# Gram products of two heads issued in turn into two PSUM banks, and a task order planned with other durations

## The chip, the core and the metric

The kernel runs on one core of one Trainium2 chip. The metric is the device time of one execution in microseconds. Three runs of the kernel before took 3414.15, 3416.99 and 3423.1 us; the median is 3416.99.

## The reference, cut to what matters

Two layers over 512 latent tokens with 256 context tokens in front, width 1024. Layer 0 mixes by attention and convolution, layer 1 by RWKV-7, a recurrence over the tokens that runs once in each direction for 16 heads of 64 channels:

```python
def wkv_scan(state0, r, decay, k, a_vec, b_vec, v, reverse):
    def step(S, inp):
        r_t, w_t, k_t, a_t, b_t, v_t = inp
        sa = jnp.einsum('bhvk,bhk->bhv', S, a_t)
        S = S * w_t[:, :, None, :] + sa[..., None] * b_t[:, :, None, :] + v_t[..., None] * k_t[:, :, None, :]
        return S, jnp.einsum('bhvk,bhk->bhv', S, r_t)
```

The decay, k, a and b come out of small products (LoRA: 64 inner channels), sigmoids and exponentials of the layer's input. After the recurrence a readout with a group norm, a bonus term and a gate follows, and then a feed-forward block.

## The kernel before, in words

The kernel does the recurrence in chunks of 32 tokens, 24 chunks in each direction (8 of the context, 16 of the latent tokens). It goes in three steps: projections; a preparation (`rwkv_prep`) that needs no state; and the scan over the chunks (`rwkv_scan`). The change lies in the preparation.

The preparation works on 16 units u = 2m + d: m is one of 8 pairs of heads, d the direction. A pair of heads fills the 128 partitions: the first head (par = 0) has partitions 0 to 63, the second (par = 1) 64 to 127. For each pair it loads k and r (L2030, L2031) and normalises k (kk, L2044); for each unit it does the following.

- Two LoRA products into PSUM (pool `psa`), a tanh of each on ACT (L2070), a running sum over the tokens on DVE (`scan`, L2079 and L2081), and exponentials on ACT.
- DVE builds two tiles of 128 x 24 chunks x 64: `AR` (the decayed a and r, L2123 and L2127) and `KB` (the inversely decayed k and b, L2138 and L2142).
- TensorE forms for each head and chunk the 64 x 64 product of KB's chunk with AR's: the gram tiles (`gram`). One call fills one bank of `psa` with 12 chunks of one head: 6 side by side, and the two halves hf of the chunks on the two halves of the PSUM partitions. Four calls, (b, par) for b and par in 0, 1, make a unit. DVE masks each bank into the tile G (L2158).
- TensorE transposes KB (L2168, pool `psb`), ACT copies it into KT (L2171).
- AR, G and KT are spilled to DRAM by SP's queue (L2146, L2175, L2179), from where the scan loads them.

For each pair of heads there is also a bonus and gate part (L2244 to L2264) that ends in two stores to p_d (L2263, L2264); the work tiles of k, r, v and g are shared through small pools. After unit 7 a batch of triangular inverses (T, L2414 to L2483: 11 steps of rows and blocks, then 8 products and 8 sums, on DVE) starts for the first half of the heads, on what units 0 to 7 have spilled.

The order of all this is not written by hand. Every piece is a `task` with an engine (P, V, A, G, S for TensorE, DVE, ACT, GpSimd and SP), a duration in us, its dependences, what it takes and gives of the pools (`t` 15 tiles, `u` 5, `pa` and `pb` 4 banks each, `kb` and `kt` 2), a latency and a nominal unit. `run_tasks` is a list planner: it walks through time, starts on each free engine the ready task with the lowest priority number, and issues the instructions in that order. The priority is 3 times the unit, plus the earliest time by the durations, plus an offset for each kind of task from a table that stands in the call. On the chip every engine then takes its instructions in the order planned, and waits where an operand is not there.

Of the kernel before, what the change touches and what calls it, by code (L numbers as in the profile page):

```python
# [430 lines left out]
class K:  # L431
# [1534 lines left out]
    def rwkv_prep(self):  # L1966
        nc, A, dp = self.nc, self.A, self.dp
# [27 lines left out]
        def par_(n):  # L1995
            return slice(64 * n, 64 * n + 64)
# [17 lines left out]
        def tt(n):  # L2014
            return {"V": 0.1 + n / 960}

        def last(z, key, n):

# [5 lines left out]
        def head_tasks(m):  # L2024
            z = mz[m]
            u = 2 * m

            def load():
                z["k"], z["r"] = tt_("k"), tu_("r")
                nc.sync.dma_start(out=z["k"], in_=self.k_d[m])  # L2030
                nc.sync.dma_start(out=z["r"], in_=self.r_d[m])  # L2031

            def kn_p(i):
                if i == 0:
                    z["kk"] = tt_("kk")
                n = (512, 256)[i]
                ps = z["knp", i] = self.psb()
                for par in range(2):
                    h = 2 * m + par
                    self.mm(ps[par_(par), 0:n], self.cs[0:16, CC.at["ident"] + h:CC.at["ident"] + h + 1].to_broadcast([16, 64]), self.rn[i])  # L2040

            def kn_v(i):
                t0, n = ((0, 512), (512, 256))[i]
                nc.vector.scalar_tensor_tensor(z["kk"][:, t0:t0 + n], last(z, "k", 4)[:, t0:t0 + n], dcol[:, 56 + m:57 + m], z.pop(("knp", i))[:, 0:n], ALU.mult, ALU.mult)  # L2044

            task(("ld", m), "S", 1.82, load, [("bd", m - 2)], take=("t", "u"), u=u - 1, lat=2.2)
            for i in range(2):
                task(("knp", m, i), "P", (0.87, 0.45)[i], lambda i=i: kn_p(i), [("knp", m, 0), ("ld", m)], take=("pb",) + (("t",) if i == 0 else ()), u=u)
                task(("kk", m, i), "V", (0.66, 0.40)[i], lambda i=i: kn_v(i), [("knp", m, i), ("ld", m), ("cols",)], give=("pb", (("k", m), "t", 4)), u=u)

        def dir_tasks(u):
            m, d = u // 2, u % 2
# [104 lines left out]
            def gram_v(b, par):  # L2157
                nc.vector.tensor_tensor(G[:, 3 * b:3 * b + 3, par], z.pop(("g", b, par))[:, 0:384].rearrange("p (a s i) -> p a s i", a=3, s=2),  # L2158
# [21 lines left out]

            for w in "wa":
                for i in range(2):
                    task((w + "p", u, i), "P", (0.33, 0.65)[i], lambda w=w, i=i: lora_p(w, i), [(w + "p", u, 0), ("kb", u - 2)] + [("lo", 0 if w == "w" else 1), ("w2", 0 if w == "w" else 1)], take=("pa",) + (("t",) if i == 0 else ()), u=u - 0.5)
                    task((w, u, i), "A", (0.36, 0.57)[i], lambda w=w, i=i: lora_a(w, i), [(w + "p", u, i), ("cols",)], give=("pa",), u=u - 0.5, lat=0.25)
                if w == "w":
                    task(("half", u), "A", 0.83, half, [("w", u, 0), ("w", u, 1)], u=u, lat=0.25)
# [3 lines left out]
                    task(("wexp", u), "A", 1.36, wexp, [("dexp", u)], u=u, lat=0.25)  # L2190
            a = [("a", u, 0), ("a", u, 1)]
            task(("kb", u), "V", 0.87, k_b, a + kk, take=("t",), give=((("kk", m), "t", 6),), u=u)
            task(("kf", u), "A", 0.93, k_f, [("kb", u)], u=u, lat=0.25)
            task(("kd", u), "V", tt(768)["V"], lambda: k_d(nc.vector), [("kf", u), ("ld", m)], give=((("k", m), "t", 4),), u=u)
            old = [("z", d), ("sa", u - 2)] + [("g", u - 2, b, par) for b in range(2) for par in range(2)]
            for i in range(2):
                task(("ma", u, i), "V", (0.36, 0.66)[i], lambda i=i: mk_a(i), [("wexp", u)] + kk + old, give=((("kk", m), "t", 6), (("s", u), "t", 3)), u=u)
            task(("mr", u), "V", 0.64, mk_r, [("wexp", u), ("ld", m)] + old, give=((("s", u), "t", 3),), u=u)
            task(("me", u), "A", 0.2, mk_e, [("ld", m)] + old, u=u)
            ks = []  # L2200
            for i in range(len(pc)):
# [2 lines left out]
                ks.append(("mk", u, i))  # L2204
            for i in range(len(pc)):
                n = pc[i][3] - pc[i][2]
                task(("mb", u, i), "V", 0.1 + n / 960, lambda i=i: mk_b(i), [("kb", u), ("dexp", u), ("mk", u, 0)], give=((("dm", u), "t", 2 * len(pc)), (("b", u), "t", len(pc))), u=u)
# [12 lines left out]
            if u < 14:  # L2220
                task(("sk", u), "S", 2.2, spill_k, [("tc", u, b) for b in range(3)] + [("g", u, b, par) for b in range(2) for par in range(2)], give=("kt", "kb"), u=u, lat=2.2)
            else:
                self.late.append(spill_k)

        def bonus_tasks(m):
# [42 lines left out]
            task(("gp", m), "P", 0.65, gate, [("bd", m - 1), ("lo", 2), ("w2", 2)], take=("pb", "u"), u=u - 1)  # L2268
            task(("gc", m), "A", 0.48, gate_c, [("gp", m)], give=("pb",), u=u - 1, lat=0.25)
            task(("ba", m), "V", tt(512)["V"], lambda: add(nc.vector), ks, give=("t",), u=u)  # L2270
            task(("bm", m), "V", 0.66, mul, [("ba", m)] + [(n, 2 * m + d) for d in range(2) for n in ("mr", "me")], give=("t",), u=u)
            task(("bd", m), "P", 0.86, dot, [("bm", m)], take=("pb",), give=("u",), u=u)
            task(("b1", m), "V", 0.6, o1, [("bd", m), ("vl", m)], give=("pb",), u=u)
            task(("b2", m), "V", 0.66, o2, [("b1", m), ("gc", m)], u=u)
            task(("b3", m), "A", 0.61, o3, [("b2", m)], u=u, lat=0.25)
# [61 lines left out]
        for m in range(8):  # L2337
# [6 lines left out]
        self.run_tasks(tasks, dict(t=15, u=5, kb=2, kt=2, e2=2, pa=4, pb=4, raw=4, hi=1), eng, 3, 1.07, {'scan': -46.0, 'ld': -16.9, 'mask': -3.9, 'cols': -10.7, 'mr': -4.5, 'mb': -9.4, 'knp': -10.2, 'b1': 1.3, 'ap': -1.0, 'bs': 8.0, 'kk': -2.8, 'wp': -2.0, 'ba': -6.5, 'gc': -32.9, 'lh': 6.0, 'dexp': -2.2, 'll': -18.4, 'kb': -0.8, 'w2': 1.9, 'half': -4.7, 'vl': -11.4, 'kf': -0.1, 'gp': 3.9, 'z': -16.1, 'sg': -51.3, 'b3': -0.2, 'sa': 17.7, 'tp': -10.9, 'a': 0.9, 'lo': 34.2, 'T': 3.5, 'bd': -7.6, 'sk': 3.9, 'dm': 58.8, 'g': -8.5, 'b2': 3.0, 'mk': 0.4, 'wexp': -0.1, 'ma': -0.1, 'gv': -0.4, 'w': -0.4, 'bm': -0.2, 'tc': -0.1, 'kd': 1.6})  # L2344
        for u in (14, 15):
            del us[u]["KB"]
        w2.clear()
# [731 lines left out]
```

## Time and profile before

| what | value |
|---|---|
| median of three runs | 3416.99 us |
| profiled execution | 3418.43 us, span 3416.6 us |
| mean granted TensorE clock over the span | 0.937 |
| PE, DVE, ACT, POOL busy over the span | 92%, 65%, 34%, 14% |
| the preparation (read from the timeline) | from about 2415 us to about 2660 us of the span |
| gram instructions in it | 1536, 67.65 us busy |

Times in the profile are microseconds from the start of the span. An fp32 product shows as two MATMUL rows, so the 768 gram products are 1536 rows. PE busy is the time in which at least one product is in flight; products on different parts of the array can be in flight at the same time. The granted clock is 1.0 or 0.5 at any moment; a mean between them is a share of time.

### The profile page before, as it was taken

Reading aid. Unit: us, or ns where it says so; the run is one execution under the profiler, and the core shown is the slowest. Engines: PE = TensorE matmul, PEld = TensorE weight load, DVE = VectorE, ACT = ScalarE, POOL = GpSimd, SP = SyncE. Lnnn points to the kernel's source line nnn. Section 1 sums busy time; section 2 is a strip of 40 time slices with the busy share of each in tenths; the row PEclk is TensorE's granted clock in tenths of the full one; section 3 lists DMA queues with packets and bytes.
Section 4 is the critical chain, followed back from the end, with each engine's and each line's share of the span. In section 5 each row is a group of like instructions: output and inputs, shape, how many; then the busy total and the mean of one; then the engine's idle time right before and its main releaser. Section 6 shows DMA issues by size and latency. Waiting matters only on the chain. (4 is left out here: it accounts for less than half of the span.)

```text
span 3416.6 us, 53235 instructions
## 1 busy us (share of the span) xinstructions
PE 3157.3 (92%) x21616; PEld 2654.6 (78%) x21616; DVE 2215.4 (65%) x3658; ACT 1175.8 (34%) x2130; POOL 468.6 (14%) x362
## 2 busy tenths in 40 slices
PE   7999999988999999999999999998996478899999
PEld 6888888874578888888889988776665367678887
DVE  5877744797666776555767776637778675653433
ACT  4122113445533111213322323434654245532222
POOL 1000001366320000002000000216000142220000
PEclk9999999999999999999999999999755688989999
DMA  6444311200133444431111111232686888732222
GB/s 242 144 149 154 133 62 62 85 25 1 44 104 122 143 145 148 145 121 50 62 67 64 68 62 66 96 111 69 194 219 187 191 181 185 175 125 97 99 99 80
DMA packets 251382, 390.69 MB, mean 114 GB/s; under 512 B 67328, under 2 KB 136576, under 8 KB 251136
## 3 DMA queue, kind: packets, MB, share of 16 engines
q1 hardware_dynamic: 251136, 387.28, 36.7%
q8 instruction: 170, 2.79, 0.3%
q14 instruction: 76, 0.62, 0.1%
HBM read 323.24 MB, written 63.96 MB: 113 GB/s over the span
## 5 line engine op out<-in xcount | busy, mean ns | idle before, releaser
L528 PE MATMUL psa<-hhi,whi 128*128 128x512 f32 (+2 forms) x2296 | 797.1, 347 | 9.2 <-ACT whi L492 3.9
L528 PE MATMUL psa<-hlo,whi 128*128 128x512 f32 (+2 forms) x2296 | 798.1, 348 | 2.5 <-POOL hlo L680 2.3
L528 PE MATMUL psa<-hhi,wlo 128*128 128x512 f32 (+2 forms) x2296 | 795.7, 347 | 0.0
L499 DVE TENSOR_TENSOR wlo<-wraw,whi 128x1024 fp32r<-128x1024 f32 (+2 forms) x246 | 301.1, 1227 | 308.3 <-ACT whi L492 308.3
L528 PEld LDWEIGHTS psa<-hhi,whi 128*128 128x128 f32 x2296 | 436.1, 190 | 62.2 <-ACT whi L492 3.9
L528 PEld LDWEIGHTS psa<-hlo,whi 128*128 128x128 f32 x2296 | 435.7, 190 | 56.6 <-POOL hlo L680 4.2
L528 PEld LDWEIGHTS psa<-hhi,wlo 128*128 128x128 f32 x2296 | 435.9, 190 | 48.7
L528 PE MATMUL psb<-ghi,whi 128*128 128x256 f32 (+1 forms) x1232 | 428.7, 348 | 15.6 <-DVE xb L814 12.4
L528 PE MATMUL psb<-glo,whi 128*128 128x256 f32 (+1 forms) x1232 | 426.8, 346 | 0.9 <-DVE glo L377 0.2
L528 PE MATMUL psb<-ghi,wlo 128*128 128x256 f32 (+1 forms) x1232 | 426.0, 346 | 0.0
L492 ACT CAST whi<-wraw 128x1024 fp32r<-128x1024 f32 (+3 forms) x293 | 290.0, 1000 | 255.2 <-PE psb L528 103.7
L637 POOL TENSOR_TENSOR nacc<-nacc,nsq 128x512 f32<-128x512 f32 (+1 forms) x50 | 56.4, 1128 | 1576.1 <-ACT nsq L633 1571.2
L528 PEld LDWEIGHTS psb<-ghi,whi 128*128 128x128 f32 x1232 | 232.8, 189 | 49.0 <-DVE xb L814 13.8
L528 PEld LDWEIGHTS psb<-glo,whi 128*128 128x128 f32 x1232 | 232.7, 189 | 30.6 <-DVE glo L377 3.3
L528 PEld LDWEIGHTS psb<-ghi,wlo 128*128 128x128 f32 x1232 | 232.7, 189 | 29.9
L786 ACT CAST ghi<-fs 128x256 fp32r<-128x256 f32 (+1 forms) x118 | 63.0, 534 | 419.0 <-DVE fs L785 419.0
L777 ACT ACTIVATE fs<-psa 128x256 f32<-128x256 f32 (+1 forms) x116 | 59.5, 513 | 419.0 <-PE psa L528 419.0
L814 DVE SCALAR_TENSOR_TENSOR xb<-psb,mod,xb 128x256 f32<-128x256 f32 (+1 forms) x256 | 148.9, 611 | 51.4 <-PE psb L528 51.3
L563 DVE CUSTOM_DVE_ANT_0 adaj<-adat,sc,vec 128x512 bf16<-128x512 f32 x224 | 168.0, 750 | 15.0 <-DMA adat<-ada 9.3
L563 DVE CUSTOM_DVE_ANT_0 adaj<-adat,sc,mod 128x512 bf16<-128x512 f32 x224 | 168.0, 750 | 5.8 <-DMA adat<-ada 0.2
L528 PE MATMUL psb<-rhs,lhs 96*32 96x64 f32 (+1 forms) x2560 | 78.9, 237 | 70.6 <-DMA rhs<-v_d 39.6
L235 DVE TENSOR_TENSOR wlo<-wraw,whi 128x1024 fp32r<-128x1024 f32 x70 | 85.6, 1223 | 89.2 <-ACT whi L232 89.2
(422 smaller groups left out, 5381.8 us busy)
## 6 DMA issues: line engine op xcount, KB each, us to landing
wraw<-w SPq DMA_DIRECT2D x242, 512.0 KB
adat<-ada SPq DMA_DIRECT2D x256, 256.0 KB
la_d<-AR SPq DMA_DIRECT2D x32, 384.0 KB
kb_d<-KT SPq DMA_DIRECT2D x16, 768.0 KB
lg_d<-G SPq DMA_DIRECT2D x32, 384.0 KB
lhs<-la_d SPq DMA_DIRECT2D x48, 256.0 KB
lhs<-lg_d SPq DMA_DIRECT2D x48, 256.0 KB
kb<-kb_d SPq DMA_DIRECT2D x48, 256.0 KB
```

What stands on the lines that cost most here:

```text
L235: TT(lo, x, hi, ALU.subtract)
L492: nc.scalar.copy(hi, raw)
L499: nc.vector.tensor_tensor(lo, raw, hi, ALU.subtract)
L528: self.last = self.nc.tensor.matmul(ps, lhsT=lhsT, rhs=rhs, start=start, stop=stop)
L563: nc.vector.tensor_tensor_reduce(out=junk, in0=t, in1=self.sc[cd][hf], scale=1.0, scalar=o if hf else self.col("ada_b", l * 72 + j), op0=A ...
L637: (eng or nc.gpsimd).tensor_tensor(st["acc"], st["acc"], sq, ALU.add)
L777: nc.scalar.activation(s, ps[:, 0:grp[1]], AF.Silu)
L786: nc.scalar.copy(ghi[:, t0:t0 + n], s)
L814: nc.vector.scalar_tensor_tensor(xs, ps[:, 0:n], self.modc(l, gd, m, cd), xs, ALU.mult, ALU.add)
```

## The change

There are two parts. `gram` now takes two banks at once, one for each head of the pair, and issues the 24 products of both heads in turn: for each chunk first the head on partitions 0 to 63, then the one on 64 to 127. The two calls of one b become one task that takes two `pa` banks; the evictions stay separate, each giving one bank back, and both depend on the joint task. The number of products, their shapes and what they write are the same.

The second part changes the durations that the planner reckons with (TensorE tasks become up to twice as long, DVE and ACT tasks about 0.1 us longer, `scan` 1.75 us and not 0.95) and replaces the table of offsets. Each engine has the same number of instructions as before.

```diff
-            return {"V": 0.1 + n / 960}
+            return {"V": 0.15 + n / 960}
...
-            def gram(b, par):
-
-                ps = z["g", b, par] = self.psa()
-                p = par_(par)
+            def gram(b):
+
+                ps = [self.psa(), self.psa()]
+                z["g", b, 0], z["g", b, 1] = ps
                 for a in range(6):
                     for hf in range(2):
                         n = 12 * hf + 6 * b + a
-                        self.mm(ps[64 * hf:64 * hf + 64, 64 * a:64 * a + 64], z["KB"][p, n, :], AR[p, n, :])
+                        for par in range(2):
+                            p = par_(par)
+                            self.mm(ps[par][64 * hf:64 * hf + 64, 64 * a:64 * a + 64], z["KB"][p, n, :], AR[p, n, :])
...
-                    task((w + "p", u, i), "P", (0.33, 0.65)[i], lambda w=w, i=i: lora_p(w, i), ...
+                    task((w + "p", u, i), "P", (0.6, 1.1)[i], lambda w=w, i=i: lora_p(w, i), ...
...
-                    task(("scan", u), "V", 0.95, scan, [("half", u), ("mask",)], take=("t",), give=("t",), u=u)
+                    task(("scan", u), "V", 1.75, scan, [("half", u), ("mask",)], take=("t",), give=("t",), u=u)
...
             for b in range(2):
+                task(("g", u, b), "P", 1.7, lambda b=b: gram(b), ks + mar, take=("pa", "pa"), u=u)
                 for par in range(2):
-                    task(("g", u, b, par), "P", 0.8, lambda b=b, par=par: gram(b, par), ks + mar, take=("pa",), u=u)
-                    task(("gv", u, b, par), "V", 0.53, lambda b=b, par=par: gram_v(b, par), [("g", u, b, par), ("sg", u - 2)], give=("pa",), u=u)
+                    task(("gv", u, b, par), "V", 0.55, lambda b=b, par=par: gram_v(b, par), [("g", u, b), ("sg", u - 2)], give=("pa",), u=u)
             for b in range(3):
-                task(("tp", u, b), "P", 0.44, lambda b=b: trans(b), ks + [("tp", u, 0)], take=("pb",) + (("kt",) if b == 0 else ()), u=u)
+                task(("tp", u, b), "P", 0.85, lambda b=b: trans(b), ks + [("tp", u, 0)], take=("pb",) + (("kt",) if b == 0 else ()), u=u)
...
-        self.run_tasks(tasks, dict(t=15, ...), eng, 3, 1.07, {'scan': -46.0, 'ld': -16.9, 'mask': -3.9, ...})
+        self.run_tasks(tasks, dict(t=15, ...), eng, 3, 1.07, {'scan': -31.6, 'ld': -101.4, 'mask': -96.3, ...})
```

Three places of the new order follow. The lines of the changed kernel are two higher from the gram task on.

TensorE, the first two gram tasks of unit 0 (AR_20696 is the AR tile of direction 0, AR_20697 of direction 1; lh and ll are LoRA inputs; rows with KB and cs are the transposes). Before:

```order
L2168 MATMUL psb<-cs,KB 128x128 x4
L528 MATMUL psa<-lh_20715,whi 128x256
L528 MATMUL psa<-ll_20716,whi 128x256
L528 MATMUL psa<-lh_20715,wlo 128x256
L2168 MATMUL psb<-cs,KB 128x128 x8
L528 MATMUL psa<-AR_20696,KB 64x64 x48
L2168 MATMUL psb<-cs,KB 128x128 x12
L528 MATMUL psa<-AR_20697,KB 64x64 x48
```

Now:

```order
L528 MATMUL psa<-AR_20696,KB 64x64 x24
L528 MATMUL psa<-lh_20717,whi 128x256
L528 MATMUL psa<-ll_20718,whi 128x256
L528 MATMUL psa<-lh_20717,wlo 128x256
L2170 MATMUL psb<-cs,KB 128x128 x4
L528 MATMUL psa<-lh_20717,whi 128x512
L528 MATMUL psa<-ll_20718,whi 128x512
L528 MATMUL psa<-lh_20717,wlo 128x512
L528 MATMUL psa<-AR_20696,KB 64x64 x24
```

The 48 products of unit 0 stood in one run, a head at a time, behind its transposes. Now they come in two runs of 24, each of both heads, before and between the transposes, with LoRA products of other units in between.

SP's queue, around the load of k and r of the last pair of heads (the only L2030 and L2031 rows here). Before:

```order
L2179 DMA kb_d<-KT 128x12x128
L2175 DMA lg_d<-G_20699 64x6x256 x2
L2263 DMA p_d<-g 128x512
L2264 DMA p_d<-v 128x512
L2263 DMA p_d<-g 128x512
L2264 DMA p_d<-v 128x512
L2030 DMA k<-k_d 128x768
L2031 DMA r<-r_d 128x512
L2233 DMA v<-vt_d 128x512
L2146 DMA la_d<-AR_20696 64x12x128 x2
```

Now:

```order
L2146 DMA la_d<-AR_20696 64x12x128 x2
L2181 DMA kb_d<-KT 128x12x128
L2030 DMA k<-k_d 128x768
L2031 DMA r<-r_d 128x512
L2181 DMA kb_d<-KT 128x12x128
L2177 DMA lg_d<-G_20699 64x6x256 x2
L2146 DMA la_d<-AR_20697 64x12x128 x2
L2265 DMA p_d<-g 128x512
L2266 DMA p_d<-v 128x512
```

The load stood behind the p_d stores of pairs 5 and 6, and now stands ahead of both, with spills of units 11 to 13 between.

DVE, the last steps of the batch of triangular inverses (prod, tinv, tw) among the last units' work. Before (its last steps stand between the G rows of units 14 and 15, near the end of the preparation):

```order
L2158 TENSOR_TENSOR G_20698<-psa,cs 128x3x128 x2
L2478 TENSOR_REDUCE tinv<-prod 128x16x4
L2158 TENSOR_TENSOR G_20699<-psa,cs 128x3x128
L2474 TENSOR_TENSOR prod<-tw,tinv 128x1024
L2158 TENSOR_TENSOR G_20699<-psa,cs 128x3x128 x3
L2478 TENSOR_REDUCE tinv<-prod 128x16x4 x3
L2254 TENSOR_TENSOR v<-psb,v 128x512
```

Now (the KB rows are those of units 14 and 15):

```order
L2476 TENSOR_TENSOR prod<-tw,tinv 128x1024
L2127 TENSOR_TENSOR AR_20697<-r,s 128x16x31
L2160 TENSOR_TENSOR G_20699<-psa,cs 128x3x128 x2
...
L2480 TENSOR_REDUCE tinv<-prod 128x16x4 x3
L2114 TENSOR_TENSOR a<-a,k 128x768 x2
L2138 TENSOR_TENSOR KB<-a,dm 128x24x32
L2142 SCALAR_TENSOR_TENSOR KB<-b,dm 128x24x32
```

The batch ended behind the last unit's gram evictions and now ends before the last two units' KB tiles are built. Counted in DVE's 287 tasks it ran from the 199th to the 285th, and now runs from the 177th to the 267th.

More of the change, by code (lines that the diff above doesn't have):

```diff
@@ L2047, in head_tasks @@
             for i in range(2):
-                task(("knp", m, i), "P", (0.87, 0.45)[i], lambda i=i: kn_p(i), [("knp", m, 0), ("ld", m)], take=("pb",) + (("t",) if i == 0 else ()), u=u)
-                task(("kk", m, i), "V", (0.66, 0.40)[i], lambda i=i: kn_v(i), [("knp", m, i), ("ld", m), ("cols",)], give=("pb", (("k", m), "t", 4)), u=u)
+                task(("knp", m, i), "P", (0.95, 0.5)[i], lambda i=i: kn_p(i), [("knp", m, 0), ("ld", m)], take=("pb",) + (("t",) if i == 0 else ()), u=u)
+                task(("kk", m, i), "V", (0.74, 0.48)[i], lambda i=i: kn_v(i), [("knp", m, i), ("ld", m), ("cols",)], give=("pb", (("k", m), "t", 4)), u=u)
         def dir_tasks(u):
@@ L2182, in dir_tasks @@
                 for i in range(2):
-                    task((w + "p", u, i), "P", (0.33, 0.65)[i], lambda w=w, i=i: lora_p(w, i), [(w + "p", u, 0), ("kb", u - 2)] + [("lo", 0 if w == "w" else 1), ("w2", 0 if w == "w" else 1)], take=("pa",) + (("t",) if i == 0 else ()), u=u - 0.5)
-                    task((w, u, i), "A", (0.36, 0.57)[i], lambda w=w, i=i: lora_a(w, i), [(w + "p", u, i), ("cols",)], give=("pa",), u=u - 0.5, lat=0.25)
+                    task((w + "p", u, i), "P", (0.6, 1.1)[i], lambda w=w, i=i: lora_p(w, i), [(w + "p", u, 0), ("kb", u - 2)] + [("lo", 0 if w == "w" else 1), ("w2", 0 if w == "w" else 1)], take=("pa",) + (("t",) if i == 0 else ()), u=u - 0.5)
@@ L2185, in dir_tasks @@
+                    task((w, u, i), "A", (0.47, 0.69)[i], lambda w=w, i=i: lora_a(w, i), [(w + "p", u, i), ("cols",)], give=("pa",), u=u - 0.5, lat=0.25)
                 if w == "w":
-                    task(("half", u), "A", 0.83, half, [("w", u, 0), ("w", u, 1)], u=u, lat=0.25)
-                    task(("scan", u), "V", 0.95, scan, [("half", u), ("mask",)], take=("t",), give=("t",), u=u)
+                    task(("half", u), "A", 0.94, half, [("w", u, 0), ("w", u, 1)], u=u, lat=0.25)
+                    task(("scan", u), "V", 1.75, scan, [("half", u), ("mask",)], take=("t",), give=("t",), u=u)
@@ L2188, in dir_tasks @@
                     task(("dm", u), "G", 0.2, dm, [("half", u)], take=("t",), u=u)
                     task(("dexp", u), "A", 0.83, dexp, [("scan", u), ("dm", u)], u=u, lat=0.25)
-                    task(("wexp", u), "A", 1.36, wexp, [("dexp", u)], u=u, lat=0.25)
+                    task(("wexp", u), "A", 1.5, wexp, [("dexp", u)], u=u, lat=0.25)
             a = [("a", u, 0), ("a", u, 1)]
-            task(("kb", u), "V", 0.87, k_b, a + kk, take=("t",), give=((("kk", m), "t", 6),), u=u)
-            task(("kf", u), "A", 0.93, k_f, [("kb", u)], u=u, lat=0.25)
+            task(("kb", u), "V", 0.95, k_b, a + kk, take=("t",), give=((("kk", m), "t", 6),), u=u)
@@ L2194, in dir_tasks @@
+            task(("kf", u), "A", 1.02, k_f, [("kb", u)], u=u, lat=0.25)
             task(("kd", u), "V", tt(768)["V"], lambda: k_d(nc.vector), [("kf", u), ("ld", m)], give=((("k", m), "t", 4),), u=u)
-            old = [("z", d), ("sa", u - 2)] + [("g", u - 2, b, par) for b in range(2) for par in range(2)]
+            old = [("z", d), ("sa", u - 2)] + [("g", u - 2, b) for b in range(2)]
             for i in range(2):
-                task(("ma", u, i), "V", (0.36, 0.66)[i], lambda i=i: mk_a(i), [("wexp", u)] + kk + old, give=((("kk", m), "t", 6), (("s", u), "t", 3)), u=u)
@@ L2198, in dir_tasks @@
[L2198 removed]
+                task(("ma", u, i), "V", (0.42, 0.68)[i], lambda i=i: mk_a(i), [("wexp", u)] + kk + old, give=((("kk", m), "t", 6), (("s", u), "t", 3)), u=u)
+            task(("mr", u), "V", 0.67, mk_r, [("wexp", u), ("ld", m)] + old, give=((("s", u), "t", 3),), u=u)
             task(("me", u), "A", 0.2, mk_e, [("ld", m)] + old, u=u)
@@ L2220, in dir_tasks @@
             if u < 14:
-                task(("sk", u), "S", 2.2, spill_k, [("tc", u, b) for b in range(3)] + [("g", u, b, par) for b in range(2) for par in range(2)], give=("kt", "kb"), u=u, lat=2.2)
+                task(("sk", u), "S", 2.2, spill_k, [("tc", u, b) for b in range(3)] + [("g", u, b) for b in range(2)], give=("kt", "kb"), u=u, lat=2.2)
             else:
@@ L2267, in bonus_tasks @@
             task(("vl", m), "S", 0.75, v_load, [("ld", m), ("bd", m - 1)], take=("u",), u=u - 1.5, lat=2.2)
-            task(("gp", m), "P", 0.65, gate, [("bd", m - 1), ("lo", 2), ("w2", 2)], take=("pb", "u"), u=u - 1)
-            task(("gc", m), "A", 0.48, gate_c, [("gp", m)], give=("pb",), u=u - 1, lat=0.25)
+            task(("gp", m), "P", 1.3, gate, [("bd", m - 1), ("lo", 2), ("w2", 2)], take=("pb", "u"), u=u - 1)
+            task(("gc", m), "A", 0.58, gate_c, [("gp", m)], give=("pb",), u=u - 1, lat=0.25)
             task(("ba", m), "V", tt(512)["V"], lambda: add(nc.vector), ks, give=("t",), u=u)
[L2271 to L2275, printed above, removed]
+            task(("bm", m), "V", 0.75, mul, [("ba", m)] + [(n, 2 * m + d) for d in range(2) for n in ("mr", "me")], give=("t",), u=u)
+            task(("bd", m), "P", 1.0, dot, [("bm", m)], take=("pb",), give=("u",), u=u)
+            task(("b1", m), "V", 0.69, o1, [("bd", m), ("vl", m)], give=("pb",), u=u)
+            task(("b2", m), "V", 0.75, o2, [("b1", m), ("gc", m)], u=u)
+            task(("b3", m), "A", 0.71, o3, [("b2", m)], u=u, lat=0.25)
             if m < 7:
```

4 lines of the change are left out of this document (2 added, 2 removed).

## The prediction

> **What bounds the kernel now.** I read the page first, for where the stage of the change lies and what TensorE's clock does there (40 slices of 85.4 us; tenths of busy time and of full clock):
>
> ```profile
> span 3416.6 us, 53235 instructions
> ...
> PE   7999999988999999999999999998996478899999
> PEclk9999999999999999999999999999755688989999
> ```
>
> From about 2415 us the granted clock falls to about half, while PE stays at 8 to 9 tenths: that is the preparation. The sums over stretches cut it in two at 2610 us (columns: length, busy time and instructions of PE, weight loads, DVE, ACT and POOL, mean clock, DMA share, GB/s):
>
> ```profile
> 2415.00:2610.00 195.00, 182.45 (x1684) 131.12 (x1684) 151.42 (x232) 123.80 (x240) 4.02 (x18) 0.57 0.74 201
> 2610.00:2660.00 50.00, 19.76 (x344) 15.90 (x341) 45.66 (x68) 10.22 (x18) 5.70 (x4) 0.70 0.65 174
> ```
>
> In the first stretch PE is busy 93.6% of the time at a mean clock of 0.57 and DVE 77.7%; in the second DVE is busy 91.3% and PE 39.5%. So PE bounds 195 us, DVE the last 50, and no engine is full over all 245 (DVE sums to 197.1, PE to 202.2). The chain of waits over 2415 to 2660 says how much of that sets the end:
>
> ```profile
> by line: PE psa L528 32.3%; PE psb L2168 10.6%; PE psb L528 10.0%; issue 5.8%; DVE G L2158 3.9%; DMA r<-r_d 3.7%; DMA p_d<-g 3.4%; DMA v<-vt_d 2.9%; DVE b L2107 2.5%; DVE KB L2138 1.6%; DVE KB L2142 1.5%; DVE prod L2463 1.3%; DVE prod L2474
> ```
>
> PE holds 52.9% of the chain. What DVE waits for in the first stretch is PE, directly or through ACT:
>
> ```profile
> DVE kk L2044 <- PE psb L528: 8.8, 7, 4.3
> DVE s L2079 <- ACT w L2073: 8.2, 5, 2.1
> DVE G L2158 <- PE psa L528: 8.0, 14, 2.2
> ```
>
> **Term 1, the gram products.** All gram instructions are psa<-AR,KB; their share of the two stretches, and runs of them in the order of time (start, length, count; the first three at half clock, the last two at full clock):
>
> ```profile
> 2415.00:2610.00 195.00, 59.24 (x1248) 54.86 (x1248) 23.07 (x41) 3.04 (x14) 0.00 (x0) 0.57 0.74 201
> 2610.00:2660.00 50.00, 8.41 (x293) 7.76 (x290) 4.19 (x8) 0.34 (x2) 0.00 (x0) 0.70 0.65 174
> ...
> 2485.96 1.55 PE L528 MATMUL psa<-AR,KB 64*64 64x64 f32 x24
> 2492.47 2.47 PE L528 MATMUL psa<-AR,KB 64*64 64x64 f32 x48
> 2437.83 4.31 PE L528 MATMUL psa<-AR,KB 64*64 64x64 f32 x96
> 2515.24 0.91 PE L528 MATMUL psa<-AR,KB 64*64 64x64 f32 x24
> 2517.11 1.44 PE L528 MATMUL psa<-AR,KB 64*64 64x64 f32 x48
> ```
>
> One program-level product is two of these instructions, so 24 are the tile of one head and 48 the tiles of both. 48 take 2.47 us, less than two times 1.55: something overlaps. Looking at instants of the run of 96 that starts at 2437.83 (the count is of gram instructions in flight):
>
> ```profile
> 2438.40:2438.41 0.01, 0.01 (x6) 0.50 1.04 205
> 2438.50:2438.51 0.01, 0.01 (x6) 0.50 1.45 256
> 2439.05:2439.06 0.01, 0.01 (x12) 0.50 0.84 256
> 2439.50:2439.51 0.01, 0.01 (x6) 0.50 0.78 205
> ```
>
> Six are in flight inside one head's tile, twelve for a moment near 2439.05, where the end of the first head's tile (partitions 0 to 63) and the start of the second's (64 to 127) meet. So products on the two halves of the partitions run side by side, each at its own pace, but only across the boundary, since the order of before issues a whole tile of one half first. The change issues them in turn, into two banks, so twelve should be in flight throughout: 48 instructions in the time that 24 take alone.
>
> Price of a pair of tiles. If that happens: 1.55 us at half clock, 0.91 at full. If nothing more overlaps than in the runs of 48: 2.47 and 1.44. A mean clock of 0.57 is 86% half and 14% full. The first stretch has 1248/48 = 26 pairs, so they cost 26 x (0.86 x 1.55 + 0.14 x 0.91) = 38.0 us or 26 x (0.86 x 2.47 + 0.14 x 1.44) = 60.5 us, against 59.24 now: a gain of 21.2 us of PE, or none. I take 21.2, because the twelve in flight are measured. The other six pairs (1536 - 1248 = 288 instructions) lie where PE is idle anyway and count as nothing; that cover is gone only if PE becomes the bound there.
>
> The Trainium skill, "TensorE: Matmul & The Clock Gate", section "Wait — 56ns, not 53.3ns?", says that starts of matmuls never come closer than about 25 ns however small they are; the closest row above is 30 ns (1.44 us for 48), so no run here contradicts it. By it 48 instructions at full clock need an estimated 1.2 us and more, so the 14% at full clock would gain next to nothing, and the term would be about 19.5 us; at half clock 1.55 us for 48 is 32 ns each, which the rule allows.
>
> How much of 21.2 us reaches the end: with the chain's share, 0.53 x 21.2 = 11.2; all of it if PE stays the bound of the first stretch. DVE is no cover against it: shortened to 174 us the stretch would hold 151.4 us of DVE work, 87%, less than the 91.3% that it does in the second. I take 15.
>
> **Term 2, the planned order.** No instruction is added or removed by it; durations in the planner change, and with them the order on all queues. Two places matter. First the load of the last pair's k and r (L2030, L2031). On SP it stands behind two pairs' stores to p_d, and then TensorE, DVE and the load are in one chain:
>
> ```profile
> 2621.60 2.06 SPq L2263 DMA_DIRECT2D p_d<-g  x1
> 2623.75 1.63 SPq L2264 DMA_DIRECT2D p_d<-v  x1
> 2625.48 0.38 SPq L2263 DMA_DIRECT2D p_d<-g  x1
> 2625.96 0.54 SPq L2264 DMA_DIRECT2D p_d<-v  x1
> 2626.54 0.49 SPq L2030 DMA_DIRECT2D k<-k_d  x1
> 2627.13 0.41 SPq L2031 DMA_DIRECT2D r<-r_d  x1
> ...
> 2631.73 1.26 DVE L2127 TENSOR_TENSOR AR<-r,s 128x496 f32<-128x496 f32 x2 [2.03 <-DMA r<-r_d]
> ...
> 2641.51 1.11 PE L2168 MATMUL psb<-cs,KB 128*128 128x128 f32 x4 [21.06 <-DVE KB L2142]
> ```
>
> PE stands idle for 21.06 us, and the last two units' whole work starts at 2631.73. In the new order that load precedes both pairs' stores, with la_d and lg_d spills between. Second, DVE fills that hole with the triangular-inverse batch, all of it late; its rows in the second stretch:
>
> ```profile
> L2474 DVE TENSOR_TENSOR prod<-tw,tinv 128x256 f32<-128x256 f32 (+3 forms) x4 | 5.4, 1352 | 0.0
> L2463 DVE TENSOR_TENSOR prod<-tinv,lt 128x1024 f32<-128x1024 f32 (+3 forms) x4 | 4.8, 1242 | 0.0
> L2467 DVE TENSOR_REDUCE tw<-prod 128x64 f32<-128x768 f32 (+3 forms) x4 | 3.1, 816 | 0.0
> L2478 DVE TENSOR_REDUCE tinv<-prod 128x64 f32<-128x256 f32 (+3 forms) x4 | 3.1, 801 | 0.0
> L2446 DVE TENSOR_TENSOR prod<-tv,tinv 128x512 f32<-128x512 f32 x2 | 2.0, 1070 | 0.0
> L2454 DVE TENSOR_REDUCE tv<-prod 128x64 f32<-128x512 f32 x2 | 1.3, 684 | 0.0
> L2454 DVE TENSOR_REDUCE tinv<-prod 128x64 f32<-128x512 f32 x2 | 1.3, 684 | 0.0
> ```
>
> These are 21.0 us. The new order starts the batch 22 tasks earlier and ends it 20 tasks before DVE's last, not 2. DVE has 195 - 151.4 = 43.6 us idle in the first stretch, of which term 1 takes 15: 28.6 are left, so at most all 21.0 us go there, and at least none, if each step finds DVE busy. About a third of the batch still lies among the last units' work, and idle pieces are short, so I take 7. Queues passed: SP's next rows wait less or as long; nothing is moved on POOL. Earlier loads meet a fuller DMA, now at a share of 0.74; the same bytes in 223 us, not 245, are 0.79 on average, and I count nothing for it.
>
> Each pair now holds two of the four psa banks until both evictions are done, and the first eviction waits for both heads. LoRA products share these banks. One eviction is 0.55 us:
>
> ```profile
> L2158 DVE TENSOR_TENSOR G<-psa,cs x64: 536/551/559, 2443.3 to 2654.6; 128x384 f32<-128x384 f32 x64
> ```
>
> If every pair of the first stretch delayed PE by one, that would be 26 x 0.55 = 14.3 us; below nothing it cannot go. PE now has work of other units queued behind, so I count none in the sum and keep 14.3 for the range.
>
> **Sum.** 15 + 7 = 22 us off the profiled execution's 3418.43 us (its span of 3416.6 and 1.8 around it) gives 3396.4. The median of the runs is 3416.99, 1.4 lower: 3395.0. Check: a stage of 245 - 22 = 223 us holds DVE's 197.1 at 88%, between its 80% now and the 91.3% of the last stretch.
>
> **Rivals.**
> (a) DVE runs at 91.3% throughout, which its own second stretch shows possible: the stage is 197.1/0.913 = 216 us, 29 less, 3388. For it: the waits above are PE's. Against: the fill-in at 2415 and short dependences.
> (b) Only the grams gain, by the chain's share, and the order gives nothing: 11.2 less, 3405.8. For it: 5.8% of the chain is issue and 10% is DMA (r, p_d, v), which no cheaper gram touches.
> (c) The change doesn't do what it says: the banks give back 14.3 of term 1's 15 and the order helps no more; 0.7 less, 3416. For it, G already waits for PE 14 times in the first stretch. The Trainium skill, "TensorEngine Tiling (Array Packing)", section "PSUM Bottleneck", says the same in general: tiling speeds the products, and the copies out of PSUM may become the limit. Against it: two evictions are 1.1 us, less than a pair's 1.55.
> (d) Slower: the full-clock stretches vanish. These are nearly all of them in the stage:
>
> ```profile
> 2445.00:2459.00 14.00, 12.68 (x151) 0.99 0.96 257
> 2510.00:2524.00 14.00, 12.25 (x170) 0.99 0.93 259
> ...
> 2646.00:2657.00 11.00, 6.80 (x183) 0.97 0.64 154
> ```
>
> At half clock PE's work there takes up to twice as long: 24.9 us more in the first stretch, against a gram gain at half clock of 59.24 - 26 x 1.55 = 18.9, so 6.0 worse, and 6.8 in the last: 12.8 us slower, 3430. It decides from about 19 of the 31.7 us of full-clock work lost. For it: a busy PE alone does not keep the clock (93.6% busy at 0.57), and shorter grams leave more holes. Against: twice as many products in flight is more activity, not less.
>
> **How the numbers follow.** The forecast (12 to 28 off) gets 0.45, (a) 0.17, (b) 0.17, (c) 0.12, (d) 0.09. This kernel's measurement tells about 0.3%, 10.3 us, from no change. Faster by that: the forecast and (a), and half of (b) = 0.70. Same: the rest of (b) and (c) = 0.21; slower: (d), 0.09. The range goes from 3377 (DVE at 96%, 205 us: 40 off) to 3416 (case (c)); what lies outside is (d), half of (c) and a little below.
>
> **What would show it.** Right: a run of 48 gram instructions takes 1.5 to 1.7 us at half clock, with twelve in flight inside it; their sum falls from 67.6 (59.24 + 8.41) to about 45 us; no PE wait of 20 us for KB near the end; DVE at 86% or more over a stage of 223 us. Wrong: runs of 48 still at 2.4 us; a PE that waits for G or an ACT copy before each pair; a mean clock near 0.50; or the hole back in another place, behind a load or a store on SP. Outside the stage every stretch should keep its length.

## The result, and the profile after

The changed kernel takes 3398.35 us (median of four runs, 3392.56 to 3401.11) against 3416.82 us before (four runs beside them, 3414.15 to 3423.1): a ratio of 0.9941 with an interval of 0.9922 to 0.996, or 18.5 us less: a small change, but clear of 1. The forecast was 3395, within 3377 to 3416. The profiled execution took 3401.11 us, its span is 17.3 us shorter than that of before. Page of the changed kernel, the span, PE and its clock in 40 slices of 85 us:

```profile
span 3399.3 us, 53233 instructions
...
PE   7999999988999999999999999999885477799999
...
PEclk9999999998999999999999999999766789999999
```

The three slices that held 7, 5 and 5 tenths of clock now hold 7, 6 and 6. The sums over stretches of the changed kernel (columns as in the prediction; cut at 2580 us here, where DVE becomes full):

```profile
2415.00:2580.00 165.00, 136.10 (x1442) 88.66 (x1443) 132.32 (x207) 106.83 (x206) 2.86 (x15) 0.65 0.79 216
2580.00:2645.00 65.00, 34.51 (x584) 25.81 (x584) 64.44 (x93) 25.73 (x53) 6.08 (x7) 0.70 0.72 192
```

The same two stretches for the gram instructions alone (psa<-AR,KB; under DVE and ACT stands what else touches AR):

```profile
2415.00:2580.00 165.00, 27.71 (x1056) 24.69 (x1056) 22.05 (x39) 2.72 (x13) 0.00 (x0) 0.65 0.79 216
2580.00:2645.00 65.00, 13.21 (x480) 11.97 (x480) 5.10 (x9) 0.64 (x3) 0.00 (x0) 0.70 0.72 192
```

PE's sum in the stage falls from 202.2 to 170.6 us, the grams' from 67.65 to 40.92. DVE keeps its work (196.8) and is busy 80.2% in the first stretch (132.32 of 165), 99.1% in the second. Two runs of 48 gram instructions from PE's timeline, the first at half clock and the second at full:

```profile
2435.15 1.56 PE L528 MATMUL psa<-AR,KB 64*64 64x64 f32 x48
2512.15 0.93 PE L528 MATMUL psa<-AR,KB 64*64 64x64 f32 x48
```

Instants inside two such runs, with the number of gram instructions in flight:

```profile
2435.70:2435.71 0.01, 0.01 (x12) 0.50 0.17 51
2515.60:2515.61 0.01, 0.01 (x16) 1.00 2.10 819
```

A run that took 2.47 and 1.44 us takes 1.56 and 0.93, with twelve to sixteen in flight where there were six. The profile models the ends of matmuls, so the lengths of the runs are firmer than the counts in flight.

What is waited for in the stage, DVE's rows of the changed kernel and then PE's (us in total, times, longest):

```profile
DVE kk L2044 <- DMA k<-k_d: 8.1, 2, 4.4
DVE AR L2127 <- DMA la_d<-AR: 6.0, 2, 3.2
DVE s L2079 <- ACT w L2073: 4.2, 2, 3.0
DVE kk L2044 <- PE psb L528: 3.3, 3, 1.6
DVE G L2160 <- PE psa L528: 2.9, 3, 1.7
...
PE psa L528 <- DVE KB L2142: 34.5, 5, 12.4
PE psa L528 <- DVE G L2160: 14.0, 7, 3.5
```

DVE's waits for PE have shrunk (kk from 8.8 to 3.3, G from 10.2 to 2.9 over the whole stage), and its two longest are now for transfers. PE waits for DVE: 34.5 us for KB and 14.0 us for a bank that an eviction must free. The rows of before for G, KB and the bank; the last stood at a third of what it is now:

```profile
DVE G L2158 <- PE psa L528: 10.2, 15, 2.2
...
PE psb L2168 <- DVE KB L2142: 25.9, 5, 21.1
PE psa L528 <- DVE G L2158: 4.6, 5, 1.2
```

**Where the 17.3 us lie.** I divide each trace by three events: the end of the last product of the projections, the end of the last gram eviction (the last G row on DVE), and the first product of the scan. "Stage" is from the first to the second, "hand-over" from the second to the third. The rows of G's eviction in the changed kernel (durations, then the first and the last start):

```profile
L2160 DVE TENSOR_TENSOR G<-psa,cs x64: 520/548/561, 2438.4 to 2643.5; 128x384 f32<-128x384 f32 x64
```

The first scan product of the changed kernel, and then that of before, in PE's timeline:

```profile
2659.25 0.65 PE L528 MATMUL psb<-rhs,lhs 96*32 96x64 f32 x16 [14.18 <-DMA rhs<-v_d]
```

```profile
2675.70 0.66 PE L528 MATMUL psb<-rhs,lhs 96*32 96x64 f32 x16 [22.90 <-DMA rhs<-v_d]
```

Before: the stage runs from 2410.7 to 2655.1 (the last G row starts at 2654.6), 244.4 us, and the hand-over 20.6. After: from 2414.0 to 2644.05, 230.1 us, and 15.2. So the stage gives 14.3 us and the hand-over 5.4; 3.3 are lost ahead of the stage (its start lies between 2408.8 and 2416.7 in the fourteen traces, whose code is the same there), and the scan and what follows give 0.9.

### The profile page after: what moved, and what is told of

Same layout as the page of the kernel before. It is cut to its first block, busy times and chain, and to the rows that moved or that the text cites. A ratio compares the mean times of both kernels' runs of the same rounds, so it can differ in the third digit from the quotient of the medians.

```text
span 3399.3 us, 53233 instructions
## 1 busy us (share of the span) xinstructions
PE 3122.7 (92%) x21616; PEld 2618.7 (77%) x21616; DVE 2214.3 (65%) x3658; ACT 1173.3 (35%) x2130; POOL 467.2 (14%) x362
## 5 line engine op out<-in xcount | busy, mean ns | idle before, releaser
L528 PE MATMUL psb<-ghi,whi 128*128 128x256 f32 (+1 forms) x1232 | 428.7, 348 | 15.7 <-DVE xb L814 12.4
L777 ACT ACTIVATE fs<-psa 128x256 f32<-128x256 f32 (+1 forms) x116 | 59.4, 512 | 417.9 <-PE psa L528 417.9
L785 DVE TENSOR_TENSOR fs<-fs,psa 128x512 f32<-128x512 f32 (+1 forms) x113 | 65.1, 576 | 117.4 <-PE psa L528 113.7
```

What stands on the lines that cost most here:

```text
L528: self.last = self.nc.tensor.matmul(ps, lhsT=lhsT, rhs=rhs, start=start, stop=stop)
L777: nc.scalar.activation(s, ps[:, 0:grp[1]], AF.Silu)
L785: nc.vector.tensor_tensor(s, s, ps[:, 0:n], ALU.mult)
```

## Experiments

All traces were divided in this way. "Gram" is the busy time of gram instructions; "full" is the time at full clock between 2412 and 2640 us, which is 228 x (2c - 1) for a mean clock c, since only 0.5 and 1.0 occur (c has two places, so it is good to 2 us); PE and DVE are busy time in the stage. The ratio is that of the timed runs to the kernel before, timed beside them.

| kernel | ratio (interval) | stage | hand-over | gram | PE | DVE | full |
|---|---|---|---|---|---|---|---|
| before | 1 | 244.4 | 20.6 | 67.6 | 202.6 | 194.3 | 41 |
| before, a second profile | 1 | 240.7 | 20.7 | 66.1 | 201.3 | 194.1 | 41 |
| changed | 0.9941 (0.9922 to 0.996) | 230.1 | 15.2 | 40.9 | 169.9 | 196.3 | 73 |
| changed, again | 0.9935 (0.9923 to 0.9947) | 227.3 | 14.7 | 42.5 | 167.3 | 196.0 | 73 |
| order only | 0.9952 (0.9937 to 0.9966) | 243.8 | 13.3 | 69.7 | 207.2 | 198.8 | 41 |
| order only, again | 0.9959 (0.9944 to 0.9974) | 242.2 | 13.0 | 68.1 | 203.6 | 198.9 | 41 |
| heads in turn, order of before | 0.9947 (0.9935 to 0.9959) | 229.3 | 20.8 | 37.2 | 160.5 | 193.0 | 96 |
| heads in turn, old planner numbers | 0.9940 (0.9928 to 0.9952) | 228.3 | 21.4 | 42.2 | 164.0 | 193.4 | 87 |
| T store last | 0.9953 (0.9935 to 0.9971) | 227.4 | 21.3 | 42.7 | 168.9 | 196.1 | 73 |
| LoRA with one product | 0.9908 (0.9883 to 0.9934) | 219.6 | 14.2 | 43.0 | 143.6 | 195.9 | 82 |
| two parts on GpSimd | 0.9933 (0.9917 to 0.995) | 227.5 | 14.8 | 41.4 | 164.9 | 197.3 | 91 |
| halves outermost | 0.9925 (0.9902 to 0.9947) | 228.1 | 14.8 | 59.4 | 169.6 | 196.4 | 109 |
| halves outermost, again | 0.9927 (0.991 to 0.9944) | 227.5 | 14.3 | 60.4 | 171.2 | 196.5 | 105 |
| LoRA in turn as well | 0.9942 (0.9927 to 0.9958) | 227.9 | 13.9 | 37.0 | 148.7 | 196.3 | 100 |

Two profiles of one kernel differ by up to 3.7 us in the stage (before: 244.4 and 240.7). The stretch for "full" leaves out the last 10 to 15 us of the longer stages: over its whole stage the kernel before has some 50 us at full clock in both profiles, the order alone 42 and 45, the changed kernel 76 and 70.

### The changed kernel again, and each part alone

The changed kernel was timed again beside three divisions of it: its order with the products one head after the other; its products with all else in the order of before (the joint gram task at the place of the second head's); and its products planned by the old durations and the old table.

```diff
 order only, in gram(b):
-                for a in range(6):
-                    for hf in range(2):
-                        n = 12 * hf + 6 * b + a
-                        for par in range(2):
-                            p = par_(par)
+                for par in range(2):
+                    p = par_(par)
+                    for a in range(6):
+                        for hf in range(2):
+                            n = 12 * hf + 6 * b + a
 heads in turn, order of before, in the planner (SEQ is the order that it finds for the kernel before):
-        while todo:
...
+        order = [(by[k], e, 0) for e, k in SEQ]
 heads in turn, old planner numbers: the kernel before with the changed gram and
+                task(("g", u, b), "P", 1.6, lambda b=b: gram(b), ks + mar, take=("pa", "pa"), u=u)
```

> The changed kernel again, beside the others of this group. Every theory expects the ratio of its first timing, 0.994 (0.992 to 0.996), about 3397 to 3400 us, with the gram instructions at about 41 us busy and a preparation of about 230 us.

> The changed kernel with its new task order, its joint gram task and its two banks, but the 24 products are issued one head after the other, as before. My theory (the two parts add, 15 us by the products in turn and 7 by the order): about 7 us under the kernel before, 3410, with gram back at 60 us or more and PE bound again for most of the stage. Rival 1 (the products alone carry the gain, the order gives nothing): no gain, 3417. Rival 2 (the order alone carries it, because DVE is full for the last 60 us and hides what PE takes): 3398 to 3401, as the changed kernel.

> The products of both heads in turn in two banks, but every engine's other work in exactly the order of the kernel before; the joint product task stands where the second head's stood. My theory: 15 us under the kernel before, 3402, with PE waiting about 20 us for the last KB as before. Rival 1 (products alone): as the changed kernel, 3398. Rival 2 (order alone): within 3 us of the kernel before, 3414 to 3417, with shorter gram runs turned into longer PE waits for DVE.

> The products in turn as a joint task of 1.6 us in the planner, with the old durations and the old table of offsets; the planner makes a third order of its own. My theory: between the exact old order and the changed kernel if the table tolerates the change, 3398 to 3403. Rival 1: 3398. Rival 2 (only the new order is good): 3414 or slower, since the table was fitted to other tasks. If it is much slower than the exact old order, the order alone is worth as much as the products.

The products in turn shorten the stage by 15.1 us (229.3; 11.4 against the second profile of before) with the order of before untouched, and leave the hand-over at 20.8. The order alone leaves the stage as it was (243.8) and shortens the hand-over by 7.3 us. Sums over the same 228 us, of before, of the order alone and of the products alone (heads in turn, order of before):

```profile
2412.00:2640.00 228.00, 191.30 (x1806) 137.43 (x1806) 181.32 (x273) 131.61 (x253) 4.02 (x18) 0.59 0.73 202
```

```profile
2412.00:2640.00 228.00, 194.41 (x1806) 137.13 (x1806) 188.02 (x281) 131.57 (x252) 4.03 (x18) 0.59 0.74 201
```

```profile
2412.00:2640.00 228.00, 160.52 (x2024) 109.16 (x2024) 192.32 (x292) 133.00 (x259) 8.53 (x21) 0.71 0.77 210
```

The order alone does bring DVE work forward: 188.0 us by 2640, not 181.3. Yet the last gram eviction comes hardly earlier (by 0.8 us), so that work was not what set it. In the timed runs each part alone is worth 0.48% and 0.53%, and both together 0.65%, less than the sum. In the profiles the changes of stage and hand-over, against the first profile of before, are 7.9 and 14.9 us alone; together they are 19.7 by the first profile of the changed kernel and 23.0 by the one taken beside these, so the profiles do not show that the parts add to less. What the timed runs show of it hangs in part on the kernel before: its median beside these runs was 3424.08 us, 3 to 7 us above its others (3416.82, 3420.79, 3419.77), and it counts once in each ratio. Without it, the changed kernel (3398.76) is 10.5 us under the order alone (3409.27) and 6.7 under the products alone (3405.42). Whether the parts overlap is not settled. The old planner numbers with the joint task do as well as the changed kernel (0.9940 against 0.9935, with overlapping intervals), so against this kernel the timed runs show no gain from planning with the new durations; only the traces do, at the hand-over (21.4 against 14.7).

### What the new order does at the hand-over

SP's queue at the end of the stage, before and after. Columns: start, length and count of the issues:

```profile
2650.74 5.65 SPq L2175 DMA_DIRECT2D lg_d<-G  x4
2657.79 2.98 SPq L2483 DMA_DIRECT2D t_d<-tinv  x4
2660.82 7.25 SPq L2414 DMA_DIRECT2D lt<-lg_d  x2
```

```profile
2633.61 5.63 SPq L2485 DMA_DIRECT2D t_d<-tinv  x4
...
2641.31 5.66 SPq L2177 DMA_DIRECT2D lg_d<-G  x4
2648.58 2.90 SPq L2416 DMA_DIRECT2D lt<-lg_d  x2
2651.57 1.90 SPq L2551 DMA_DIRECT2D tc<-t_d  x2
...
2654.70 0.58 SPq L2544 DMA_DIRECT2D rhs<-v_d  x1
```

The store of the triangular inverses (t_d<-tinv) stood between the last gram spills (lg_d<-G) and the loads with which the second half's inverses and the scan begin. Now it precedes the last spills. The next kernel keeps the changed kernel's order, written out as a fixed list, and moves only this store back behind the last spills:

```diff
 SEQ, SP's tasks alone and shortened (T, 0, st is the store, sg the gram spills):
-    ('S', ('T', 0, 'st')), ..., ('S', ('sg', 15)),
+    ..., ('S', ('sg', 15)), ('S', ('T', 0, 'st')),
```

> The changed kernel with one task moved: the store of the finished inverse batch (t_d<-tinv, four DMAs) goes from ahead of the last gram spills to behind them on SP, where the kernel before has it. Theory: the order's whole share of the gain lies at the hand-over to the scan. In the profiles the time from the last gram eviction to the scan's first product is 20.6 us before and 15.2 changed, and 13.3 with the order alone; there the store's 3.0 us of issue and a load of lg_d behind it that takes 7.2 and not 2.9 us stand in a row. So this run gives back 6 to 7 us: hand-over near 21 us, 3405. Rival (the hand-over is shorter because less is left to do on DVE and DMA, not because of the store's place): within 2 us of the changed kernel.

Its SP queue, and its first scan product:

```profile
2640.80 4.58 SPq L2276 DMA_DIRECT2D lg_d<-G  x4
2645.78 3.92 SPq L2546 DMA_DIRECT2D t_d<-tinv  x4
2649.74 7.06 SPq L2477 DMA_DIRECT2D lt<-lg_d  x2
...
2665.40 0.66 PE L627 MATMUL psb<-rhs,lhs 96*32 96x64 f32 x16 [20.29 <-DMA rhs<-v_d]
```

The hand-over is back at 21.3 us with the stage at 227.4: this one store is the hand-over's gain. It takes 3.9 us itself, and the load behind it takes 7.1 us to issue, as before (7.25), not 2.9. In the trace of the products alone, where the store also comes directly ahead of the load, it took 7.18, with the old planner numbers, which leave the store there too, 6.81 (hand-over 21.4), and in the second profile of before 6.79; in both traces of the order alone, where spills lie between, 4.0. Why the load is slower to issue directly behind that store is not shown. In the timed runs the difference of 6 us (0.9953 against 0.9935) is not shown, since the two intervals overlap.

### Does PE still set the end of the stage?

One kernel takes PE work away from the changed kernel in its own fixed order: it leaves out two of the three products of every LoRA. A second, in the same order, moves DVE work to GpSimd. A third saves PE time by pairing more products, in an order planned anew:

```diff
 LoRA with one product:
-                self.mm3(ps[:, 0:n], [((w2[j][0][p, ms], w2[j][1][p, ms]), (lo_t[j][0][p, t0:t0 + n], lo_t[j][1][p, t0:t0 + n]))])
+                self.mm(ps[:, 0:n], w2[j][0][p, ms], lo_t[j][0][p, t0:t0 + n])
 two parts on GpSimd (with the eight multiplications of the inverse batch, tasks ("T", 0, "w" and "x")):
-            task(("ba", m), "V", tt(512)["V"], lambda: add(nc.vector), ks, give=("t",), u=u)
+            task(("ba", m), "V", tt(512)["V"], lambda: add(nc.gpsimd), ks, give=("t",), u=u)
 LoRA in turn as well (one task for both directions, two banks, order planned anew), shortened:
+                for q, (x, y) in enumerate(((0, 0), (0, 1), (1, 0))):
+                    for e in range(2):
+                        p = par_(e)
+                        self.mm(ps[e][:, 0:n], w2[j][x][p, ms], lo_t[j][y][p, t0:t0 + n], start=(q == 0), stop=(q == 2))
```

> The changed kernel, same order, with two of the three products of every decay and a LoRA left out (the correction terms of the split operands), so that TensorE has 128 of these products fewer in the preparation. Theory (after the change DVE and its dependences bound the preparation, PE no more): the stage from the last mixing product to the last gram eviction stays at 225 to 230 us and PE only idles more. Rival (PE still bounds the first 165 us, where it is busy 82%): PE loses some 40 us of work at a mean clock of 0.65, and the stage shortens by 10 us or more.

> The changed kernel, same order, with 16 DVE instructions done by GpSimd: the eight additions of the bonus (128x512, 0.68 us on DVE each, 5.5 us) and the eight multiplications with tw or into tw of the inverse batch (10.2 us on DVE). Theory (DVE bounds the stage, above all its last 60 us, where it is busy all the time): 8 to 15 us faster than the changed kernel, about 3387. Rival 1 (chains of dependences bound, and GpSimd takes longer for each than DVE): no gain or some us slower, with DVE waits for POOL in the trace. Rival 2 (PE or DMA bound): within 2 us.

> The changed kernel, and the LoRA products of the two directions of a pair of heads (partitions 0 to 63 and 64 to 127) issued in turn into two banks, in the same way as the gram products; task order planned anew for it. Theory (PE still sets part of the end after the change: with 25 us of PE work left out the stage became 8 to 10 us shorter): PE's sum over the stage falls by 20 us or more, the stage by 5 to 10 us, to about 3390. Rival (DVE's 196 us and the DMA waits of loads and spills bound the stage now): within 3 us of the changed kernel.

With one LoRA product PE's work falls by some 25 us and the stage by 8 to 10 us (219.6 against 227.3 and 230.1, 7.7 to 10.5): PE still sets a part of the end, a third to two fifths of what it is relieved of. That the stage would stay at 225 to 230 us, as expected, did not come. LoRA in turn takes away nearly as much of PE's time (148.7 us are left), and yet the stage gains nothing (227.9), where 5 to 10 us were expected. Its order is another, and in it DVE waits more than twice as long for a spilled AR tile as in the changed kernel (6.0 us, above):

```profile
DVE AR L2236 <- DMA la_d<-AR: 13.3, 4, 7.5
```

That can account for 7 of the missing 8 to 10 us, but no run tried it apart. So what sets the end of the stage, beside a part of PE's work, is not shown.

Moving DVE work to GpSimd did not relieve DVE, and the 8 to 15 us expected of it did not come. The group of KB's second product in the changed kernel, and in this one with GpSimd's additions (the mean of eight each):

```profile
L2142 DVE SCALAR_TENSOR_TENSOR KB<-b,dm 128x768 f32<-128x768 f32 x8 | 7.5, 943 | 0.0
```

```profile
L2241 DVE SCALAR_TENSOR_TENSOR KB<-b,dm 128x768 f32<-128x768 f32 x8 | 11.8, 1479 | 0.0
...
L2345 POOL TENSOR_TENSOR a<-a 128x512 f32<-128x512 f32 x8 | 18.2, 2277 | 37.4 <-DVE a L2213 26.1 <-DVE KB L2237 10.5 <-ACT w L2169 0.8
```

The sums of this kernel:

```profile
2412.00:2640.00 228.00, 165.11 (x2022) 112.03 (x2023) 197.74 (x283) 133.21 (x258) 44.26 (x38) 0.70 0.79 211
```

15.7 us of work left DVE (5.5 for the additions in the trace of before, and 5.4 and 4.8 for the multiplications by the prediction's rows), but DVE's sum in the stage stays at 197.3 us: what remains takes longer beside GpSimd, some 14 us more over the groups that both kernels share. It is a few instructions that pay. Five of the eight in the row above take 0.94 to 0.95 us as before, and three take 1.97, 1.98 and 3.14, all beside a GpSimd instruction, which is then slow too (its additions take from 1.26 to 4.93 us):

```profile
2469.30 4.93 POOL L2345 TENSOR_TENSOR a<-a 128x512 f32<-128x512 f32 x1
...
2473.09 1.97 DVE L2241 SCALAR_TENSOR_TENSOR KB<-b,dm 128x768 f32<-128x768 f32 x1
```

The Trainium skill, "SBUF — State Buffer", section "Who interferes with whom", says that DVE and GpSimd share a pair of SBUF ports under an exclusive lock. These rows agree: an instruction with two SBUF inputs goes from 0.95 to 1.97 us beside GpSimd, and the GpSimd addition from 1.26 to 4.93 us.

### What if only two quarters of the array work at a time?

The change puts neighbouring products on different partitions of the inputs (the heads) and of the output (hf). This kernel keeps the heads in turn but does all of one half hf first:

```diff
-                for a in range(6):
-                    for hf in range(2):
+                for hf in range(2):
+                    for a in range(6):
```

> The changed kernel with the loop over the two halves of the PSUM partitions outside: the heads still alternate, but six chunks of one half of the output partitions come before the six of the other. Theory (each quarter of the array, a half of the input partitions with a half of the output partitions, runs its own products one after the other, and up to four run side by side): only two quarters are busy at a time, so a run of 48 gram instructions takes 2.5 us and more at half clock, as in the kernel before, and six are in flight. Rival (only the halves of the input partitions matter): 1.56 us as in the changed kernel.

Its second run was beside a second run of the order alone and a second profile of the kernel before:

> The kernel before, for a second profile of it. Every theory expects a stage of 244 us and a hand-over of 20 us. On the clock: if the order of the heads sets how long TensorE gets the full clock (50 us of the stage in the first profile, 42 with one head after the other in the new order, 70 to 109 in the seven profiles with the heads in turn), it shows 60 us or less; if that is chance from one execution to another, anything between 40 and 110.

> The new order with one head after the other, a second time, beside the loop with the halves outside. If the clock goes with the heads in turn: under 60 us of full clock in the stage, a stage of 240 us or more and 3408 to 3412. If chance set the first profile: a stage between 228 and 244 us.

> The heads in turn, but one half of the output partitions after the other, a second time. Its runs of 48 gram instructions take 2.47 us at half clock, as long as with one head after the other, so six products are in flight in both; in the first profile it was still as fast as the changed kernel, with 109 us of full clock. If the clock goes with the heads in turn: again 80 us or more of full clock, a stage under 235 us and a time 8 us or more under the run with one head after the other. If only the products side by side bring the gain: a stage of 240 us or more, and no difference between the two.

Runs of 48 gram instructions in its second profile, at half and at full clock:

```profile
2434.48 2.47 PE L528 MATMUL psa<-AR,KB 64*64 64x64 f32 x48
2448.22 1.44 PE L528 MATMUL psa<-AR,KB 64*64 64x64 f32 x48
```

Gram instructions in flight at two instants of the first of these:

```profile
2435.00:2435.01 0.01, 0.01 (x6) 0.50 0.17 51
2435.50:2435.51 0.01, 0.01 (x8) 0.50 0.00 0
```

The sums of this profile:

```profile
2412.00:2640.00 228.00, 171.64 (x2013) 124.19 (x2013) 195.60 (x297) 132.27 (x255) 8.40 (x22) 0.73 0.78 211
```

And the second profile of the order alone, where one head's products follow the other's:

```profile
2412.00:2640.00 228.00, 191.52 (x1831) 135.49 (x1835) 189.64 (x285) 129.82 (x251) 4.03 (x18) 0.59 0.75 202
```

A run of 48 takes 2.47 and 1.44 us as before the change, with six to eight in flight: heads in turn on one output half overlap no more than one head on two output halves. Only all four quarters at once give twelve to sixteen. And yet this kernel is as fast as the changed one (0.9925 and 0.9927), its stage as short (228.1, 227.5), its PE sum as small (171.2). What differs from the order alone is the clock: 0.73, not 0.59, so 105 us at full speed and not 41. The two kernels differ in the order of these two loops and the head loop alone, and timed beside each other they took 3394.41 and 3404.74 us. Of the 32.4 us between their PE sums (203.6 and 171.2) the grams are 7.7; the rest lies in PE work that is the same in both.

So PE's sum falls to about 170 us in either of two ways: the grams overlap (40.9, with 73 us of full clock) or they do not (60.4, with 105 us). In all ten profiles with the heads in turn the full-clock time is 73 to 109 us, in all four with one head after the other some 41. What in the alternation brings the clock is not shown, and no run separates the two effects in the changed kernel itself.

## Why the prediction was right, and where its steps were not

- **The sum**: 22 us were forecast off the profiled execution; 17.3 came in the profiles and 18.5 in the medians. The forecast holds, and so does the first term's price of a pair. Of the two terms' sizes a part is luck, as follows.
- **Term 1, the price of a pair** (1.55 and 0.91 us): measured 1.56 and 0.93, with twelve in flight and more. The gram sum is 40.9, not about 45, since more of the stage ran at full clock. The rule of the Trainium skill weighed there, "TensorE: Matmul & The Clock Gate", section "Wait — 56ns, not 53.3ns?", would have had an estimated 1.2 us and more at full clock; 48 in 0.93 us are 19 ns each, so it does not hold for products on four quarters of the array. The mean of 30 ns on which the prediction found it uncontradicted hid that single starts came 6 to 7 ns apart in pairs in the kernel before already.
- **Term 1, what reaches the end** (15 of 21.2): 14.3 in the stage of the changed kernel, 15.1 with the order of before. The number is right, in part by luck: its reason is incomplete. The term held the mean clock at 0.57, and it rose: PE's sum fell by 32.7 us, more than the grams' 26.7, with more of the stage at full clock. With the halves outermost the price of a pair stays as before, and the stage is as short by the clock. The stage fell by less than half of what PE's sum lost, and DVE now fills 85% (196.3 of 230.1). The check said 88% over 223 us.
- **Term 2, the order** (7): the size is about right, 5.4 in the changed kernel and 7.3 and 7.6 alone, but that is luck, since the place is wrong. The step that failed is "so at most all 21.0 us go there ... I take 7". Batch work did move into DVE's earlier time (188.0 us by 2640, not 181.3), but the stage did not end earlier for it. The gain is behind the stage, where the prediction costed nothing ("SP's next rows wait less or as long"): the store at the batch's end no longer stands between the last spills and the load. I had looked at what DVE does in the hole and not at which DMA the batch ends in.
- **The hole at the load of the last pair** (21.06 us): it went as forecast, but came back in smaller pieces. PE waits 12.4 and 9.5 us for KB near the end, now behind a DVE that is full:

```profile
2618.78 0.48 PE L528 MATMUL psa<-AR,KB 64*64 64x64 f32 x4 [12.42 <-DVE KB L2142]
...
2635.48 2.84 PE L528 MATMUL psa<-AR,KB 64*64 64x64 f32 x96 [9.49 <-DVE KB L2142]
```

- **The banks**: counted at none, with 14.3 us as the bound. PE's waits for an eviction grew from 4.6 us (five times) to 14.0 us (seven times), the longest from 1.2 to 3.5. The stage gained its 14.3 all the same; what these waits cost was not tried apart.
- **The rivals**: (a), DVE at 91.3% throughout, is reached only in the last 65 us (99.1%). (b) had the chain's share of the grams (11.2) and nothing from the order; both are more. (c) is excluded by the stage. (d), a lost clock, went the other way: the full-clock time rose from 41 to 73 us (over the whole stages from 50 to 76).

## What to carry to other kernels

Where many small products of one kind follow each other, order them so that neighbours use different halves of the input partitions and of the output partitions (here with a bank for each head; one bank for both was not tried); then look at the granted clock as well as at the products, since either can carry the gain. In a planned order, follow each batch to the store that it ends in: here a store between the last spills and the next stage's first loads cost more than its own length. Before moving work from DVE to GpSimd, look at what the instructions that stay on DVE take beside it.

## What the runs showed of the hardware

- The granted clock depended on the order of the heads, not on how busy PE was: 41 us of 228 at full speed with one head after the other at 191 to 194 us of PE work, 105 us with the heads in turn at 172 us and hardly more gram instructions in flight. The two kernels differ in the loops of the gram products alone. In the second profile of the order alone PE is busy without a gap from 2437.2 to 2471.2 us, and the clock stays at 0.50.
- Two quarters of the array kept six to eight instructions in flight, whether the two differ in the input half or in the output half, and four kept twelve to sixteen: 48 took 2.47 and 1.56 us at half clock, 1.44 and 0.93 at full.
- GpSimd needed 1.26 to 4.93 us for an fp32 addition of 128 x 512, 2277 ns in the mean, and DVE's instructions with two SBUF inputs beside it took up to 3.14 us and not 0.95; their mean rose by 57% (943 to 1479 ns).
- The issue of one load (two DMAs) on SP's queue took 6.8 to 7.25 us directly behind the four stores of the inverses and 2.9 to 4.0 us with spills between.
